# The mixer of a two-layer streaming encoder: queries, keys and convolution input turned by transposing DMAs in place of TensorE transposes

## The chip, the core and the metric

The kernel runs on one core of a Trainium2 chip. The metric is the time of one execution on the device, in microseconds (us). Times come from the device and from a hardware profile of one execution. The engines are named as in the profile: PE is TensorE, DVE is VectorE, ACT is ScalarE, POOL is GpSimd, SP is SyncE, the queue that issues nearly all DMAs here.

## What is computed

The input x has 256 tokens of 1024 features in float32. Two layers follow one another. Each layer adds half a SwiGLU block, then a mixer, then another half SwiGLU block, each with an RMS norm before and after it. The mixer has two groups of heads side by side, whose outputs are joined and projected:

```python
def _diff_attention(q, k, v, lam_vecs, subln_g, lam_init):
    ...
    q = _rope(q, S) * (DA_HEAD_DIM ** -0.5)
    k = _rope(k, S)
    ...
        s = jnp.einsum('bhcqd,bhckd->bhcqk', q_blk, k)
        ...
        p = jax.nn.softmax(jnp.where(mask, s, -jnp.inf), axis=-1)
        a = p[:, :, 0] - lam * p[:, :, 1]
        return jnp.einsum('bhqk,bhkd->bhqd', a, v)
...
def _mlstm(qk, v, o, gates, conv_w, conv_b, gate_b, norm_g):
    ...
    qk = jax.nn.silu(_causal_conv(qk, conv_w, conv_b))
    q, k = jnp.split(qk, 2, axis=-1)
```

The differential attention has 4 heads with two score maps of 64 features each. The mLSTM group convolves its q and k over 4 tokens back, and then does gated linear attention in chunks with a carried state.

What matters for the change: the projections come out with tokens on the partitions. The attention scores need q and k with features on the partitions, and so does the convolution, which shifts along tokens. So 128x128 blocks of q and k (after the rotary embedding) and of the convolution's input are turned between the projections and their use.

## The kernel before, in words

All matrix products are done in three passes on split operands (each float32 operand is a rounded high part plus a low part, `mm3`, L401 to L403). Weights are streamed: a piece of 1 MB is loaded by SP into one of three buffers `wr` (L282), and each of its two halves is split by ACT (`wh`, L288) and DVE (`wl`, L289). A buffer is free for the next load once the second half's L289 is done.

In the SwiGLU blocks the hidden activation is turned by a DMA already (`ffn_planes`, L530): ACT sorts the 16-bit halves of 128x512 floats into two planes (`planes`, L535), SP issues one transposing DMA of the planes (`turned`, L537), DVE interleaves the halves again (`hT`, L539). This happens 40 times.

The mixer (`mixer`, L703) computes six projections of 512 columns: convolution input, q, k, the mLSTM values, the attention values, the output gate, each for two tiles of 128 tokens (t = 0, 1). `traverse` (L773) writes out the order by hand: the projections are cut into 84 steps of three matmuls, and at each step the stages of the attention and mLSTM that are due there are put ahead of it. The table `AT` gives the step of each entry of the list in `stages` (L829). The order in which a step's instructions are emitted sets the order on PE; on ACT, DVE and SP a scheduler then places the instructions by their estimated times. Each engine works through its own list in order, and an instruction that waits holds up all behind it.

The turns of the mixer before the change are four 128x128 transposes on PE into a PSUM bank (`transposed`, L875, L879), and one copy out of it by ACT:

- `conv_input` (L889) evacuates the convolution's input to `nat`; `conv_input_t` (L898) turns it into `xpad`, at L899. Twice for each mixer.
- `rope` (L1052) evacuates a projection to `rv` with the norm's factor (L1057) and rotates it on DVE: `ra` = rv*cos (L1058), `rb` = swapped rv*sin (L1063), `ra` += `rb` (L1064). `roped` (L1067) turns `ra` into `qkT` at L1071, with the factor 0.125 for q. Four times for each mixer: q for t = 0, 1, then k for t = 0, 1.

These stages take part in what follows:

- `gate_rows` (L967): four PE transposes of `g2`, which DVE writes at L957; the scan `gate_chain` (L973) follows on DVE, then the convolution on DVE (L910).
- `weighted_qk` (L1018): small matmuls on PE (L1023, L1025, L1031) into three PSUM banks; DVE then reads them: `qd` (L1028), `wem` (L1027), `kwn` (L1033).
- `scores` (L1081): 16 matmuls (L1094) into two banks, then `intra_weights` (L1045) into two more. Both come from a ring of four banks called `bk`, the one that `weighted_qk` uses: the second bank of the scores, in this ring, is the one that `qd` reads.
- DVE fills the masked part (L1097) and takes the maximum (L1098), ACT takes the exponential, `combine` (L1110) subtracts on DVE (L1122) and turns the result on PE (L1124).

SBUF tiles named `nat`, `ra`, `rb`, `rv`, `planes`, `turned`, `hT` and some others share a ring of five buffers (tag `ev`), handed out in the order of emission.

## Time and profile before

| what | value |
|---|---|
| time, median of 3 runs | 963.02 us (962.27 to 963.16) |
| the profiled execution's own time | 962.02 us |
| its span, first to last instruction | 960.2 us |
| granted TensorE clock, mean | 0.999 of full speed |
| PE busy | 952.8 us, 99% of the span, 4523 instructions |
| DVE busy | 638.7 us, 67% |
| ACT busy | 571.2 us, 59% |
| DMA | 189.32 MB, mean 197 GB/s |

The span is 1.8 us shorter than the profiled execution's time, and that execution is 1.0 us under the median of the runs. Busy shares are averages over the whole span; the mixers of the two layers lie at about 195 to 275 us and about 669 to 749 us of it, and have shares of their own. In a profile's rows a line such as "L879 PE MATMUL" is a line of the kernel's code, the names are tiles without their buffer numbers, and a bracket at a row's end is the time the engine was idle just before the row and what ended that. A row that holds several instructions has their count behind an x; its time runs from the first one's start to the last one's end, and matmuls overlap one another, so that the time a matmul costs is read from the distance between starts.

### The profile page before, as it was taken

What the parts mean: (1) busy time and instruction counts of PE and PEld (TensorE: products, weight loads), DVE (VectorE), ACT (ScalarE), POOL (GpSimd) and SP (SyncE); (2) the same over time, 40 slices, a digit from 0 to 9 for tenths busy, and PEclk for the clock granted to TensorE, in tenths of its full rate; (3) what the DMA queues carried; (4) which work ended last, traced back from release to release, by engine and by line L of the source; (5) the groups of instructions that cost most, each with busy time, mean ns of one, the idle gap of its engine ahead of it and who ended that gap; (6) DMA issues with size and microseconds to landing.
All of it is one profiled execution on the core that took longest, in us unless ns stands there. A gap on an engine that the chain in (4) does not pass through costs nothing.

```text
span 960.2 us, 12037 instructions
## 1 busy us (share of the span) xinstructions
PE 952.8 (99%) x4523; PEld 788.9 (82%) x4523; DVE 638.7 (67%) x945; ACT 571.2 (59%) x937; POOL 29.5 (3%) x55
## 2 busy tenths in 40 slices
PE   9999999999999999999999999999999999999997
PEld 7888888888888888888888888888888888888885
DVE  6765655689867766555687555566988676755553
ACT  8755554577856655454476555555778466555542
POOL 2000000000010000000000000000001000000000
PEclk9999999999999999999999999999999999999999
DMA  8996656236352975676458666653454257765621
GB/s 317 328 288 202 225 193 219 105 132 241 116 192 91 299 245 193 218 247 176 154 189 283 206 225 208 196 187 128 172 202 174 90 182 256 272 205 192 225 72 44
DMA packets 69879, 189.32 MB, mean 197 GB/s; under 512 B 45274, under 2 KB 46426, under 8 KB 49086
## 3 DMA queue, kind: packets, MB, share of 16 engines
q1 hardware_dynamic: 69246, 187.95, 58.0%
q8 instruction: 35, 0.57, 0.2%
q10 hardware_dynamic: 576, 0.61, 0.2%
q14 instruction: 22, 0.18, 0.1%
HBM read 177.01 MB, written 1.05 MB: 185 GB/s over the span
## 4 chain that ended last, share of the span: by engine, by line
PE 97%; DVE 1%; DMA 1%; ACT 0%; issue 0%; POOLq 0%; DVEq 0%; ACTq 0%
PE pin L401 13%; PE pin L402 13%; PE pin L403 13%; PE bk L401 10%; PE bk L402 10%; PE bk L403 10%; PE ptr L402 6%; PE ptr L403 6%; PE ptr L401 6%; PE pin L610 1%; PE ptr L610 1%; PE ptr L879 1%; PE ptr L427 1%; DMA wr<-in_w_dram 1%; PE bk L1094 1%; PE ptr L615 1%
## 5 line engine op out<-in xcount | busy, mean ns | idle before, releaser
L289 DVE TENSOR_TENSOR wl<-wr,wh 128x1024 fp32r<-128x1024 f32 x324 | 389.2, 1221 | 180.4 <-ACT wh L288 174.4
L288 ACT ACTIVATE wh<-wr 128x1024 fp32r<-128x1024 f32 x324 | 333.9, 1055 | 171.2 <-DMA wr<-in_w_dram 44.1
L401 PE MATMUL pin<-wh,both 128*128 128x512 f32 x560 | 221.2, 396 | 0.0
L403 PE MATMUL pin<-wh,both 128*128 128x512 f32 x560 | 218.3, 390 | 0.0
L402 PE MATMUL pin<-wl,both 128*128 128x512 f32 x560 | 218.2, 390 | 0.0
L401 PE MATMUL bk<-wh,hh 128*128 128x512 f32 x352 | 137.4, 390 | 0.1
L402 PE MATMUL bk<-wl,hh 128*128 128x512 f32 x352 | 137.0, 389 | 0.0
L403 PE MATMUL bk<-wh,hl 128*128 128x512 f32 x352 | 136.9, 389 | 0.0
L403 PEld LDWEIGHTS pin<-wh,both 128*128 128x128 f32 x560 | 105.1, 188 | 22.3
L401 PEld LDWEIGHTS pin<-wh,both 128*128 128x128 f32 x560 | 105.3, 188 | 22.0 <-issue 0.7
L402 PEld LDWEIGHTS pin<-wl,both 128*128 128x128 f32 x560 | 105.3, 188 | 20.6
L403 PE MATMUL ptr<-wh,both 128*128 128x512 f32 x256 | 99.4, 389 | 0.0
L402 PE MATMUL ptr<-wl,both 128*128 128x512 f32 x256 | 99.4, 389 | 0.0
L401 PE MATMUL ptr<-wh,both 128*128 128x512 f32 x256 | 98.9, 389 | 0.0
L401 PEld LDWEIGHTS bk<-wh,hh 128*128 128x128 f32 x352 | 66.1, 188 | 14.0 <-ACT hh L550 0.5
L403 PEld LDWEIGHTS bk<-wh,hl 128*128 128x128 f32 x352 | 66.1, 188 | 13.7
L402 PEld LDWEIGHTS bk<-wl,hh 128*128 128x128 f32 x352 | 66.1, 188 | 13.5
L539 DVE COPY hT<-turned 128x1024 uint16<-128x1024 uint16 x40 | 30.3, 757 | 41.9 <-DMA turned<-planes 41.5
L401 PEld LDWEIGHTS ptr<-wh,both 128*128 128x128 f32 x256 | 48.1, 188 | 10.0
L402 PEld LDWEIGHTS ptr<-wl,both 128*128 128x128 f32 x256 | 48.1, 188 | 10.0
L550 ACT ACTIVATE hh<-hT 128x256 fp32r<-128x256 f32 x80 | 28.9, 409 | 46.0 <-DVE hT L539 46.0
L403 PEld LDWEIGHTS ptr<-wh,both 128*128 128x128 f32 x256 | 48.1, 188 | 9.9
(210 smaller groups left out, 891.9 us busy)
## 6 DMA issues: line engine op xcount, KB each, us to landing
wr<-in_w_dram SPq DMA_DIRECT2D x162, 1024.0 KB, 5.2
gpost<-in_gpost_dram SPq DMA_DIRECT2D x6, 512.0 KB, 6.3
wr<-in_w_dram SPq DMA_DIRECT2D x2, 512.0 KB, 6.1
wr<-in_w_dram SPq DMA_DIRECT2D x3, 256.0 KB, 4.3
x<-in_x_dram SPq DMA_DIRECT2D x3, 256.0 KB, 4.4
turned<-planes SPq DMA_TRANSPOSE x40, 4.4
out_dram<-x SPq DMA_DIRECT2D x2, 256.0 KB, 2.1
x<-in_x_dram SPq DMA_DIRECT2D x2, 128.0 KB, 3.0
```

The source lines that it names most:

```text
L288: ia = nc.scalar.activation(hi, raw[:, j], AF.Copy)
L289: iv = nc.vector.tensor_tensor(lo, raw[:, j], hi.bitcast(F32), op=ALU.subtract)
L401: mm(ps, xh, wh, start=start, stop=False)
L402: mm(ps, xh, wl, start=False, stop=False)
L403: mm(ps, xl, wh, start=False, stop=stop)
L427: nc.tensor.transpose(ptr[:, k, :], x[:, (4 * hf + k) * P:(4 * hf + k + 1) * P], self.ident)
L539: nc.vector.tensor_copy(hT.rearrange("p b n -> p (b n)").bitcast(U16).rearrange("p (n u) -> p u n", u=2), turned.rearrange("p (u b) n -> p ...
L550: self.nc.scalar.activation(hh, h, AF.Copy)
L610: self.nc.tensor.matmul(b, self.cols(w[kh], k)[0][:, c], both[kh][:, k].rearrange("p i t -> p (i t)"), start=kh == 0 and k == 0, stop=Fals ...
L615: self.nc.tensor.matmul(b[:, 0:NT * P], self.cols(w[kh], k)[1][:, c], both[kh][:, k, 0:NT].rearrange("p i t -> p (i t)"), start=False, sto ...
L879: self.T(ptr[:, b, :], a[:, b * P:(b + 1) * P], self.tr.ident)
L1094: self.mm(pcs[c][:, h, :], self.qkT[0][rows, h0 + h, t * P:(t + 1) * P], self.qkT[1][rows, h0 + h, 0:nk], start=True, stop=True)
```

## The change

The two helpers of the SwiGLU's turn become `turn` (ACT planes and the transposing DMA) and `joined` (the DVE copy that interleaves). The mixer uses them in place of the PE transposes: `conv_input` and `rope` end with `turn`, and `conv_input_t` and `roped` are now just the DVE copy into `xpad` or `qkT`. For each mixer this takes away 24 transposes on PE and 6 copies on ACT, and adds 6 plane sorts on ACT, 6 transposing DMAs on SP and 6 copies on DVE. The factor 0.125 of q moves into the evacuation at L1057, which needs a small product `rhalf` on DVE for each token tile. The new tiles `planes` and `turned` of the mixer come from the `ev` ring. Three stages move in the table: the turn of the convolution's input for t = 0 is now at step 10 (it was emitted ahead of step 0), q for t = 0 moves from 24 to 28, k for t = 0 from 43 to 46.

```diff
-AT = (0, 2, 6, 6, 7, 22, 24, 24, 24, 24, 36, 40, 24, 46, 34, 50, 43, 52, 52, 57, 61, 60, 61, 67, 67, 69, 71, 78, 74, 74, 78, 84)
+AT = (0, 2, 6, 6, 7, 10, 22, 24, 24, 24, 24, 36, 40, 28, 46, 34, 50, 46, 52, 52, 57, 61, 60, 61, 67, 67, 69, 71, 78, 74, 74, 78, 84)
...
     def ffn_planes(self, h):
-        nc = self.nc
-        planes = self.t2("planes", (P, 2, 512), U16)
-        nc.scalar.activation(planes, h.rearrange("p t j -> p (t j)").bitcast(U16).rearrange("p (n u) -> p u n", u=2), AF.Copy)
-        turned = self.t2("turned", (P, 8, P), U16)
-        nc.sync.dma_start_transpose(turned, planes.rearrange("p u n -> p (u n)"))
         hT = self.t2("hT", (P, 4, P))
-        nc.vector.tensor_copy(hT.rearrange("p b n -> p (b n)").bitcast(U16).rearrange("p (n u) -> p u n", u=2),
-                              turned.rearrange("p (u b) n -> p u (b n)", u=2))
+        self.joined(hT, self.turn(h.rearrange("p t j -> p (t j)")))
...
+    def turn(self, v):
+        planes = self.t2("planes", (P, 2, 512), U16)
+        self.nc.scalar.activation(planes, v.bitcast(U16).rearrange("p (n u) -> p u n", u=2), AF.Copy)
+        turned = self.t2("turned", (P, 8, P), U16)
+        self.nc.sync.dma_start_transpose(turned, planes.rearrange("p u n -> p (u n)"))
+        return turned
+
+    def joined(self, out, turned):
+        self.nc.vector.tensor_copy(out.bitcast(U16).rearrange("p b (n u) -> p u b n", u=2),
+                                   turned.rearrange("p (u b) n -> p u b n", u=2))
...
         m.part(0, 0, pins1[0], ws1[0])
-        m.conv_input_t(0)
...
             self.gate_rows,
+            lambda: self.conv_input_t(0),
             self.gate_chain,
...
-            lambda: self.roped(0, 0, 0.125),
+            lambda: self.roped(0, 0),
...
-        self.nat = nat
+        self.nat.append(tr.turn(nat))
 
     def conv_input_t(self, t):
-        self.act(self.xpad[:, :, 3 + t * P:3 + (t + 1) * P], self.transposed(self.nat), AF.Copy)
+        self.tr.joined(self.xpad[:, :, 3 + t * P:3 + (t + 1) * P], self.nat[t])
...
+        scale = self.r[t]
+        if len(self.rot) < NT:
+            scale = tr.small("rhalf", (P, 1))
+            self.ts(scale, self.r[t], 0.125, None, op0=ALU.mult)
         with tr.tc.high_priority():
-            self.rv = self.act(v, pin, AF.Copy, scale=self.r[t])
+            self.rv = self.act(v, pin, AF.Copy, scale=scale)
...
-        self.rot.append(a)
-
-    def roped(self, i, t, scale):
+        self.rot.append(tr.turn(a))
+
+    def roped(self, i, t):
...
-        self.act(self.qkT[i][:, :, t * P:(t + 1) * P], self.transposed(self.rot[2 * i + t]), AF.Copy, scale=scale)
+        self.tr.joined(self.qkT[i][:, :, t * P:(t + 1) * P], self.rot[2 * i + t])
```

How the lists change around the change is shown at three places, in the first layer's mixer. Behind the change the lines are those of the changed kernel: a few numbers higher. A bracket names the engines or DMA queues (DMAHW) that a row waits for.

The first place is DVE's list ahead of `qd`, which frees the bank that the scores wait for. `ra`, `rb` belong to the rotation of k for t = 1; `wl` are weight halves. Before:

```order
L1058 TENSOR_TENSOR ra_2136<-rv_2135,c_568 128x512 [waits Activation_49]
L1063 TENSOR_TENSOR rb_2137<-rv_2135,c_568 128x8x32 x2
L289 TENSOR_TENSOR wl_0_2324<-wr_2322,wh_0_2325 128x1024 [waits DMAHW4_49,PE_49,Activation_49]
L289 TENSOR_TENSOR wl_1_2334<-wr_2322,wh_1_2335 128x1024 [waits Activation_49]
L1064 TENSOR_TENSOR ra_2136<-ra_2136,rb_2137 128x512 [waits DVE_49]
L289 TENSOR_TENSOR wl_0_2409<-wr_2407,wh_0_2410 128x1024 [waits DMAHW5_49,Activation_49]
L1028 SCALAR_TENSOR_TENSOR qd<-qk,bk_2229 128x256 [waits PE_49]
```

And after, where `turned_2017` is q for t = 1, `turned_2114` and `turned_2149` are k for t = 0 and 1:

```order
L550 COPY qkT_2090<-turned_2017 128x2x4x128 [waits DMAHW1_49]
L1069 TENSOR_TENSOR ra_2140<-rv_2139,c_568 128x512 [waits DVE_49,Activation_49]
L1074 TENSOR_TENSOR rb_2141<-rv_2139,c_568 128x8x32 [waits DVE_49]
L1074 TENSOR_TENSOR rb_2141<-rv_2139,c_568 128x8x32
L1075 TENSOR_TENSOR ra_2140<-ra_2140,rb_2141 128x512 [waits DVE_49]
L289 TENSOR_TENSOR wl_1_2332<-wr_2320,wh_1_2333 128x1024 [waits Activation_49]
L550 COPY qkT_2211<-turned_2114 128x2x4x128 [waits DMAHW3_49]
L289 TENSOR_TENSOR wl_0_2407<-wr_2405,wh_0_2408 128x1024 [waits DMAHW0_49,Activation_49]
L550 COPY qkT_2211<-turned_2149 128x2x4x128 [waits DMAHW4_49]
L1035 SCALAR_TENSOR_TENSOR qd<-qk,bk_2232 128x256 [waits PE_49]
```

Three copies of turned halves, each of which waits for a DMA, now stand in this stretch ahead of `qd`, two of them close before it.

The second place is SP's list of the same stretch: before, the loads of weight pieces follow one another; after, the turns stand between them. Before:

```order
L282 DMA wr_2223<-in_w_dram 128x2048 [waits DMAHW7_49,DMAHW2_49,DVE_49]
L457 DMA gpost_2242<-in_gpost_dram 128x1024
L282 DMA wr_2322<-in_w_dram 128x2048 [waits DMAHW0_49,DVE_49]
L282 DMA wr_2407<-in_w_dram 128x2048 [waits DMAHW1_49,DVE_49]
L282 DMA wr_2500<-in_w_dram 128x2048 [waits DMAHW2_49,DVE_49]
L282 DMA wr_2642<-in_w_dram 128x2048 [waits DMAHW4_49,DVE_49]
```

After, with `turned_1968` and `turned_2017` for q and `turned_2114` and `turned_2149` for k:

```order
L282 DMA wr_2320<-in_w_dram 128x2048 [waits DMAHW1_49,DVE_49]
L546 DMA_TRANSPOSE turned_1968<-planes_1966 128x8x128 [waits Activation_49]
L282 DMA wr_2405<-in_w_dram 128x2048 [waits DMAHW2_49,DVE_49]
L546 DMA_TRANSPOSE turned_2017<-planes_2015 128x8x128 [waits DMAHW7_49,DMAHW3_49,Activation_49]
L282 DMA wr_2498<-in_w_dram 128x2048 [waits DMAHW4_49,DVE_49]
L546 DMA_TRANSPOSE turned_2114<-planes_2112 128x8x128 [waits Activation_49]
L546 DMA_TRANSPOSE turned_2149<-planes_2147 128x8x128 [waits DMAHW1_49,Activation_49]
L282 DMA wr_2640<-in_w_dram 128x2048 [waits DMAHW6_49,DMAHW5_49,DVE_49]
```

Each turn stands directly behind a load of 1 MB, and each load behind a turn waits in the list until that turn has been issued.

The third place is ACT's list from q for t = 1 to k for t = 1: `rv` is the evacuation of a projection, `wh` are weight halves, `qk` is the convolution's SiLU. Before:

```order
L1057 ACTIVATE rv_2099<-pin_2004,rs_191_1738 128x512 [waits PE_49]
L288 ACTIVATE wh_1_2251<-wr_2223 128x1024 [waits PE_49]
L1071 ACTIVATE qkT_2057<-ptr_2119 128x4x128 [waits PE_49]
L266 ACTIVATE qk<-conv_2038 128x1024 [waits DVE_49]
L1057 ACTIVATE rv_2135<-pin_2064,rs_204_1840 128x512 [waits PE_49]
```

And after, from the planes of q for t = 1 to those of k for t = 1:

```order
L544 ACTIVATE planes_2015<-ra_2006 128x1024 [waits DVE_49,Activation_49]
L1068 ACTIVATE rv_2104<-pin_2019,rs_191_1738 128x512 [waits PE_49]
L288 ACTIVATE wh_1_2254<-wr_2226 128x1024 [waits PE_49]
L288 ACTIVATE wh_0_2323<-wr_2320 128x1024 [waits DMAHW6_49,PE_49]
L544 ACTIVATE planes_2112<-ra_2105 128x1024 [waits DVE_49,Activation_49]
L1068 ACTIVATE rv_2139<-pin_2067,rs_206_1844 128x512 [waits DMAHW1_49]
L260 ACT_TABLE_LOAD
L288 ACTIVATE wh_1_2333<-wr_2320 128x1024 [waits PE_49]
L544 ACTIVATE planes_2147<-ra_2140 128x1024 [waits DVE_49,Activation_49]
```

The evacuation of k for t = 1 waited for PE alone as `rv_2135`. As `rv_2139` it waits for a DMA, DMAHW1, the same event that the copy out of `turned_2017` waits for on DVE: the buffer of the ring that it writes is that of the planes which the DMA of q for t = 1 still reads.

PE's list is the same at every place, without the 48 transposes.

More of the change, by code (lines that the diff above doesn't have):

```diff
@@ L765, in __init__ @@
         self.conved = None
-        self.rot, self.qkT, self.so, self.p = [], [], [], {}
+        self.nat, self.rot, self.qkT, self.so, self.p = [], [], [], [], {}
         self.aT, self.lsum, self.hn, self.y = [None] * NT, [None] * NT, [None] * NT, [None] * NT
```

6 lines of the change are left out of this document (3 added, 3 removed).

## The prediction

> **What bounds the kernel now.** I read the page first: the busy shares and the shares of the chain that ended last.
>
> ```profile
> PE 952.8 (99%) x4523; PEld 788.9 (82%) x4523; DVE 638.7 (67%) x945; ACT 571.2 (59%) x937; POOL 29.5 (3%) x55
> PE 97%; DVE 1%; DMA 1%; ACT 0%; issue 0%; POOLq 0%; DVEq 0%; ACTq 0%
> ```
>
> PE is busy all the time and carries the chain. So work taken off PE is worth its full time, as long as PE then waits for nothing. DVE's 67% is an average over the span, and the change works in the mixers alone. So I asked for the busy time by window, in the stretch from the convolution's input to `qd` of each mixer (columns: PE, PEld, DVE, ACT, POOL busy, clock, DMA share, GB/s):
>
> ```profile
> 198.60:238.30 39.70, 39.70 (x202) 32.96 (x202) 36.82 (x67) 30.93 (x45) 0.34 (x2) 1.00 0.50 182
> 672.30:712.00 39.70, 39.70 (x202) 32.96 (x202) 36.71 (x63) 30.91 (x44) 0.34 (x2) 1.00 0.50 182
> ```
>
> Here DVE has 39.70 - 36.82 = 2.9 us free, and the change puts six copies more on it. ACT has 8.8 us free. The two mixers agree within 0.1 us, so I work out the first and double it.
>
> **What is taken off PE.** PE's timeline around one group of four transposes:
>
> ```profile
> 218.59 0.40 PE L999 MATMUL bk<-c_mask,c_identr 128*128 128x512 f32 x1
> 218.82 0.60 PE L879 MATMUL ptr<-c,ra 128*128 128x128 f32 x4
> 219.18 0.48 PE L401 MATMUL pin<-wh,both 128*128 128x512 f32 x1
> 219.49 0.40 PE L402 MATMUL pin<-wl,both 128*128 128x512 f32 x1
> ...
> L879 PE MATMUL ptr<-c,ra x32: 270/272/273, 218.8 to 719.5; 128*128 128x128 f32 x32
> ```
>
> The next matmul starts 0.36 us after the group, and the one behind that 0.31 us later, where a matmul of this size takes 0.23 from start to start (218.59 to 218.82). A group costs 0.36 + 0.08 = 0.44 us; the two layers have 12 groups: 5.3 us. The duration in the last row, 272 ns for each transpose, would make that 48 x 0.272 = 13.1 us, but they overlap and the starts decide. The Trainium skill, "TensorE: Matmul & The Clock Gate", Part 4: PE-mode transpose, gives about 275 ns for a 128x128 transpose within a kernel; by it the gain would be an estimated 13.2 us. The trace agrees on the duration and not on what it costs. The six copies that leave ACT free nothing that PE waits for.
>
> **What is added.** The kernel makes the same turn 40 times in its SwiGLU blocks, so its parts have rows (the shapes are the same 128x512 floats; the copy's output is strided a little differently, and I take its price over):
>
> ```profile
> L535 ACT ACTIVATE planes<-h x40: 1037/1056/1059, 22.6 to 921.9; 128x1024 uint16<-128x1024 uint16 x40
> L539 DVE COPY hT<-turned x40: 746/755/768, 30.0 to 925.8; 128x1024 uint16<-128x1024 uint16 x40
> L537 SPq DMA_TRANSPOSE turned<-planes x40: 1237/1238/3697, 23.6 to 923.0; - x40
> DMA to landing us min/median/max: 2.7/4.4/8.9
> ```
>
> A turn alone is 1.06 + 2.7 + 0.76 = 4.5 us of delay at best, on three engines that are not PE, and 0.76 of it is DVE's. The DMA's landing is the part that varies. Behind a load of 1 MB it looks like this:
>
> ```profile
> 366.00 0.33 SPq L282 DMA_DIRECT2D wr<-in_w_dram  x1
> wr<-in_w_dram SPq DMA_DIRECT2D x1, 1024.0 KB, 5.2
> ...
> 367.64 1.24 SPq L537 DMA_TRANSPOSE turned<-planes  x1
> turned<-planes SPq DMA_TRANSPOSE x1, 4.6
> ```
>
> The load lands at 371.2, the turn at 372.2: 1.0 us after the load ahead of it, and not 2.7 after its issue. In SP's new list the turns stand just so, each behind a load. The Trainium skill, "VectorE: DVE Perf Modes", Rules for kernel authors, says to transpose 128x128 on TensorE where PSUM will do as the destination, which speaks against this change; by its table (The three transpose paths) a DMA transpose of 128x128 in bf16 takes 1309 ns, so eight of them in a row would be an estimated 10.5 us. The trace's 2.7 us for eight blocks shows that this sum does not hold here.
>
> **Where PE waits first: the gate rows.** DVE and PE around step 7:
>
> ```profile
> 198.85 2.36 DVE L289 TENSOR_TENSOR wl<-wr,wh 128x1024 fp32r<-128x1024 f32 x2 [0.25 <-ACT wh L288]
> 202.14 0.19 DVE L940 TENSOR_REDUCE gs<-bk 128x16 f32<-128x32 f32 x1 [0.93 <-PE bk L939]
> 203.36 1.22 DVE L289 TENSOR_TENSOR wl<-wr,wh 128x1024 fp32r<-128x1024 f32 x1 [0.24 <-ACT wh L288]
> ...
> 206.02 0.69 DVE L973 TENSOR_TENSOR_SCAN gt<-c_scan,bk 100x256 f32<-100x256 f32 x1
> ...
> 205.39 0.60 PE L967 MATMUL bk<-c,g 128*100 128x128 f32 x4
> ```
>
> DVE's list now has the copy into `xpad` ahead of the first of these rows and the second weight half (1.14 from start to start) ahead of `g2`, whose transposes PE makes at 205.39. That is 0.76 + 1.14 = 1.9 us more, less the 1.4 us of idle that the brackets show, plus the wait for the turn's landing (about 1 us, an estimate: the load ahead of it has to land). So `g2` is some 1.5 us late, and PE comes 0.44 early: it waits between 0.9 us (no wait for the landing) and 1.9, and I take 1.4. DVE's scan follows 1.0 us later than before. PE's wait here does not enter the sum by itself, since the next one is longer and takes it in.
>
> **Where PE waits last: `qd`.** The second bank of the scores is the one that `qd` must have read. Rows of PE, DVE and ACT ahead of it, and of the load that stands ahead of the turn of q for t = 1:
>
> ```profile
> 237.97 0.33 PE L1023 MATMUL bk<-eh,c_hotp 128*128 128x128 f32 x2
> ...
> 239.98 1.16 PE L1094 MATMUL bk<-qkT,qkT 64*128 64x128 f32 x16
> ...
> 226.45 1.22 DVE L289 TENSOR_TENSOR wl<-wr,wh 128x1024 fp32r<-128x1024 f32 x1
> ...
> 232.13 0.68 DVE L1058 TENSOR_TENSOR ra<-rv,c 128x512 f32<-128x512 f32 x1
> 232.73 0.75 DVE L1063 TENSOR_TENSOR rb<-rv,c 128x256 f32<-128x256 f32 x2
> ...
> 235.68 0.69 DVE L1064 TENSOR_TENSOR ra<-ra,rb 128x512 f32<-128x512 f32 x1
> ...
> 238.34 0.42 DVE L1028 SCALAR_TENSOR_TENSOR qd<-qk,bk 128x256 f32<-128x256 f32 x1 [0.84 <-PE bk L1023]
> ...
> 229.07 0.67 ACT L1057 ACTIVATE rv<-pin,rs 128x512 f32<-128x512 f32 x1
> ...
> 227.70 0.33 SPq L282 DMA_DIRECT2D wr<-in_w_dram  x1
> wr<-in_w_dram SPq DMA_DIRECT2D x1, 1024.0 KB, 4.9
> ```
>
> Before, DVE waits 0.84 us for PE at `qd`, so `qd` costs nothing. In the new lists a chain of turns ends there. In the times of this trace:
>
> - The weight half at 226.45 frees the buffer of the load that was issued at 227.70. It now comes after the late scan (1.0), two more copies (1.5) and one more small product (0.15): it starts at 229.1 and ends at 230.3, and the load is issued then and lands 4.9 later, at 235.2.
> - The turn of q for t = 1 stands behind that load in SP's list and lands 1.0 after it: 236.2.
> - The evacuation of k for t = 1, done at 229.7 before, now waits for just this landing, as its buffer holds the planes that the DMA reads: 236.2 + 0.67 = 236.9.
> - Its rotation on DVE takes 0.60 + 0.67 + 0.69 = 1.96: 238.9. Planes on ACT, 1.06: 239.9. The DMA with no load ahead of it in flight, 2.7: 242.6. Copy, 0.76, and `qd`, 0.42: 243.8. Seven handovers between engines at about 0.05 us (an estimate: the gap from the weight half's end at 227.67 to the load's issue is 0.03): 244.2.
>
> PE reaches the scores at 239.98 - 5 x 0.44 + 1.4 = 239.2, does the first bank, and waits until 244.2: 5.0 us. Against before it is 244.2 - 239.98 = 4.2 us late. The sixth group would give 0.44 back, but the next thing that PE does for attention is fed by DVE too:
>
> ```profile
> 247.32 1.14 DVE L1122 SCALAR_TENSOR_TENSOR p<-p,c 128x128 f32<-128x128 f32 x4
> ...
> 248.06 0.78 PE L1124 MATMUL ptr<-c,p 128*128 128x128 f32 x4
> ```
>
> These four transposes start while DVE still works on what they read, so they follow DVE, which is late by the same 4.2. The later loads of weights are late by no more than PE's use of them, so I cost them at nothing; a half that PE had to wait for would add to the shift, and is what is late next.
>
> Sum: 2 x 4.2 = +8.4 us on the profiled execution, 962.02 + 8.4 = 970.4. That execution is 1.0 under the median, so I predict 971.4. The gain of 5.3 is in this number: without it the shift would be larger only where PE waits, which is why it is lost.
>
> **Bounds of the unknown terms.** The turn of k for t = 1 can land 4.4 us after its issue (the median of the 40) in place of 2.7: +1.7 for each mixer, 974.8. Or the waits of the chain turn out shorter, down to DVE's own work. With six copies at 0.755 = 4.5 us against 2.9 us of room, `qd` starts at 238.34 + 1.6 = 239.9 and ends at 240.4 at the earliest: PE is 0.4 to 0.5 late, +0.9 for both mixers, 963.9.
>
> **The rivals.** Two are above, as bounds of one mechanism: only DVE's time counts (963.9; it holds if the buffer of the evacuation is free by 230 or so). The other rivals:
>
> - *The turns are hidden, and the kernel is faster.* Each copy is done by the time PE arrives, and nothing but the gate rows holds PE. The point that decides is `qd` of each mixer: done by 237.8 in these times, the groups come off PE whole, and the time is 963.0 - 5.3 = 957.7, or 960.5 with the gate wait of 1.4 in each mixer. For it speaks that a turn needs only 4.5 us. Against it: DVE's 2.9 us of room for 4.5 us of copies, which no earlier landing changes, unless copies overlap with the 0.93 and 0.84 us that are idle now and the weight halves move behind.
> - *The wait slows PE's clock.* After the last matmul the page's tail shows the clock:
>
> ```profile
> 953.23 0.39 PE L403 MATMUL bk<-wh,hl 128*128 128x512 f32 x1
> 956.00:957.60 1.60, 0.00 (x0) 0.00 (x0) 0.86 (x3) 0.00 (x0) 0.00 (x0) 1.00 0.42 155
> 957.70:960.20 2.50, 0.00 (x0) 0.00 (x0) 0.00 (x0) 0.00 (x0) 0.00 (x0) 0.50 0.30 98
> ```
>
>   PE ends at 953.6, and the granted clock is 1.00 until 957.6 and 0.50 from 957.7: some 4.1 us of idle PE halved it. My wait is 5.0 us. If the clock halves in it and stays so for as long as that took, 4.1 us of PE work take 2.1 more in each mixer: 971.4 + 4.2 = 975.6. Against it: the wait would have to be unbroken. The Trainium skill, "TensorE: Matmul & The Clock Gate", Part 1: The HAM clock gate, gives a window of about 3.4 us of idle before the clock is halved and about as long to restore it; by it the loss is an estimated 1.7 in each mixer. The trace's 4.1 us agrees with one such window and part of a second.
> - *The copies are dearer than 0.755 us*, as their output is strided by block: at twice that, the four copies that the chain to `qd` runs through (two into `xpad`, q and k of one token tile) make it 3.0 us longer in each mixer, 977.4. Only the stride speaks for it.
>
> **Chances.** The chain as told, with its landings between the two bounds: 0.58. DVE's time alone or little more: 0.17, at 963 to 966. The halved clock: 0.16, at 974 to 978. Hidden: 0.06. Dearer copies: 0.03. A measurement of this kernel can tell about 0.2%, 1.9 us, from no change: that is 961.1 to 964.9. Half of the second case falls within it. Faster is the hidden case, 0.06; same 0.09; slower 0.85. The range from 963.0 to 978.0 leaves out the hidden case, the dearer copies and the ends of the others.
>
> **What would show it.** In the changed kernel's profile, PE should wait at the scores (L1105) for `qd` in both mixers, about 5 us each, and 1 to 2 us at the gate rows; the chain of waits should show DMA `turned` and DVE; no L879 row should be left with `nat` or `ra`; the L550 copies should be near 0.76 us; the evacuation of k for t = 1 should wait for the landing of `turned`. The prediction is wrong in its mechanism if PE's wait at the scores ends under 2 us, or is released by anything but `qd`; it is wrong in size if the turn of q for t = 1 lands well before 236 of these times. A clock under 1.00 behind the wait would be the third case.

## The result, and the profile after

The changed kernel takes 979.02 us (median of 4 runs, 976.95 to 980.55); the kernel before, run beside it, 962.64 us (962.05 to 963.16). The ratio is 1.0169, with an interval of 1.0148 to 1.019. So it is 16.4 us slower, where the prediction had 8.4 us and ended its range at 978.0. The profiled execution took 979.52 us with a span of 977.5 us, 17.3 more than before. One execution of all the experiments, of `e10_dve_passes_only`, took 3428.67 us, far outside the other three of its kernel (968.70 to 970.10 us), and is left out of that kernel's median.

I read the page of the changed kernel first, as before: busy shares and the chain that ended last.

```profile
PE 956.0 (98%) x4475; PEld 788.8 (81%) x4475; DVE 647.2 (66%) x961; ACT 578.3 (59%) x937; POOL 31.5 (3%) x55
...
PE 91%; DVE 3%; DMA 3%; ACT 2%; issue 1%; POOLq 0%; DVEq 0%; ACTq 0%
```

48 matmul records are gone, and yet PE is busy for 3.2 us longer, which points to a slower clock. The chain now leaves PE for DVE, DMA and ACT. What PE waits for, in total, times and the longest:

```profile
PE pin L401 <- ACT rv L1068: 10.5, 4, 4.1
PE bk L974 <- DVE g L964: 3.8, 2, 2.8
```

No row has the scores and `qd`. PE waits at L401, the first matmul of a projection, for the evacuation of an earlier one (`rv`, by ACT), because the PSUM bank `pin` that it wants is the one that is evacuated. PE's timeline has the six waits (bracket: idle before), the matmul behind one of them, and the scores (L1105), which have none:

```profile
206.04 0.64 PE L974 MATMUL bk<-c,g 128*100 128x128 f32 x4 [1.03 <-DVE g L964]
223.38 0.79 PE L401 MATMUL pin<-wh,both 128*128 128x512 f32 x1 [4.14 <-ACT rv L1068]
223.97 0.63 PE L402 MATMUL pin<-wl,both 128*128 128x512 f32 x1
224.40 0.63 PE L403 MATMUL pin<-wh,both 128*128 128x512 f32 x1
...
238.81 0.51 PE L401 MATMUL pin<-wh,both 128*128 128x512 f32 x1 [2.06 <-ACT rv L1068]
...
247.81 1.16 PE L1105 MATMUL bk<-qkT,qkT 64*128 64x128 f32 x16
...
689.43 1.09 PE L974 MATMUL bk<-c,g 128*100 128x128 f32 x4 [2.78 <-DVE g L964]
707.28 0.79 PE L401 MATMUL pin<-wh,both 128*128 128x512 f32 x1 [3.35 <-ACT rv L1068]
721.96 0.51 PE L401 MATMUL pin<-wh,both 128*128 128x512 f32 x1 [0.92 <-ACT rv L1068]
```

Behind the wait of 4.14 us the matmuls start 0.43 us apart (223.97 to 224.40), where before it was 0.23. The windows behind the three longest waits show why (columns: PE, PEld, DVE, ACT, POOL busy, granted clock, DMA share, GB/s):

```profile
223.40:228.20 4.80, 4.80 (x12) 3.80 (x13) 4.80 (x13) 1.39 (x2) 0.00 (x0) 0.51 1.01 222
689.40:693.00 3.60, 3.57 (x12) 3.07 (x13) 2.36 (x6) 1.10 (x2) 0.00 (x0) 0.60 1.00 373
707.30:712.20 4.90, 4.90 (x12) 3.84 (x13) 4.90 (x13) 1.54 (x2) 0.00 (x0) 0.50 1.03 227
```

The granted clock is about halved there: 4.80 x 0.49 + 3.60 x 0.40 + 4.90 x 0.50 = 6.2 us of PE's work lost. Waits of 10.5 + 3.8 = 14.3 and this 6.2 make 20.5; the span grew by 17.3. The remainder, 3.2 us, is what the twelve groups gave back, less what is not in this sum: at the prediction's 0.44 us each they give 5.3, so some 2 us of loss are not followed here.

Why are the evacuations late? ACT's rows for q of t = 1 (222.64) and k of t = 1 (238.08):

```profile
217.34 2.08 ACT L914 ACTIVATE conv<-xpad,c 128x256 f32<-128x256 f32 x4 [0.68 <-DVE xpad L550]
219.32 1.04 ACT L544 ACTIVATE planes<-ra 128x1024 uint16<-128x1024 uint16 x1
220.27 1.05 ACT L266 ACTIVATE eE<-bk 128x512 f32<-128x512 f32 x2
221.34 1.28 ACT L260 ACT_TABLE_LOAD   x1
222.64 0.69 ACT L1068 ACTIVATE rv<-pin,rhalf 128x512 f32<-128x512 f32 x1
...
238.08 0.69 ACT L1068 ACTIVATE rv<-pin,rs 128x512 f32<-128x512 f32 x1 [2.00 <-DMA turned<-planes]
```

In the kernel before, ACT evacuated q of t = 1 right behind the matmuls, 7.7 us earlier and ahead of the convolution's products:

```profile
214.92 0.69 ACT L1057 ACTIVATE rv<-pin,rs 128x512 f32<-128x512 f32 x1 [0.30 <-PE pin L403]
```

In the changed kernel it stands in ACT's list behind the convolution's products, planes, two exponentials and a table load, 5.3 us of work that itself waits for DVE's copy into `xpad`. The evacuation of k for t = 1 waits 2.00 us for a turn to land, since its `rv` takes the buffer of planes that the DMA still reads. DVE's rows show the copies of q for t = 1 and k for t = 1, and `qd`:

```profile
238.08 0.74 DVE L550 COPY qkT<-turned 128x1024 uint16<-128x1024 uint16 x1 [1.09 <-DMA turned<-planes]
...
245.31 0.75 DVE L550 COPY qkT<-turned 128x1024 uint16<-128x1024 uint16 x1 [0.57 <-DMA turned<-planes]
246.17 0.42 DVE L1035 SCALAR_TENSOR_TENSOR qd<-qk,bk 128x256 f32<-128x256 f32 x1
```

`qd` is over at 246.59, 1.2 us before PE comes to the scores at 247.81. The chain that the prediction followed exists, but PE has been held up earlier, by evacuations that the turns made late.

### The profile page after: what moved, and what is told of

Read it like the earlier page. It is cut to its first block, busy times and chain, and to the rows that moved or that the text cites. A ratio compares the mean times of both kernels' runs of the same rounds, so it can differ in the third digit from the quotient of the medians.

```text
span 977.5 us, 11988 instructions
## 1 busy us (share of the span) xinstructions
PE 956.0 (98%) x4475; PEld 788.8 (81%) x4475; DVE 647.2 (66%) x961; ACT 578.3 (59%) x937; POOL 31.5 (3%) x55
## 4 chain that ended last, share of the span: by engine, by line
PE 91%; DVE 3%; DMA 3%; ACT 2%; issue 1%; POOLq 0%; DVEq 0%; ACTq 0%
PE pin L401 12%; PE pin L402 11%; PE pin L403 11%; PE bk L401 10%; PE bk L403 10%; PE bk L402 10%; PE ptr L401 6%; PE ptr L403 6%; PE ptr L402 6%; DMA turned<-planes 3%; DVE wl L289 2%; PE pin L617 2%; PE ptr L617 2%; PE ptr L427 1%; PE pin L622 1%; PE ptr L622 1%
## 5 line engine op out<-in xcount | busy, mean ns | idle before, releaser
L289 DVE TENSOR_TENSOR wl<-wr,wh 128x1024 fp32r<-128x1024 f32 x324 | 388.8, 1221 | 181.7 <-ACT wh L288 175.4
L401 PE MATMUL pin<-wh,both 128*128 128x512 f32 x560 | 223.7, 400 | 10.5 <-ACT rv L1068 10.5
L402 PE MATMUL pin<-wl,both 128*128 128x512 f32 x560 | 220.5, 394 | 0.0
L403 PE MATMUL pin<-wh,both 128*128 128x512 f32 x560 | 220.3, 393 | 0.0
L401 PE MATMUL bk<-wh,hh 128*128 128x512 f32 x352 | 137.4, 390 | 0.0
L401 PEld LDWEIGHTS pin<-wh,both 128*128 128x128 f32 x560 | 106.8, 191 | 34.6 <-ACT rv L1068 12.2
L403 PEld LDWEIGHTS pin<-wh,both 128*128 128x128 f32 x560 | 106.6, 190 | 22.9
L401 PE MATMUL ptr<-wh,both 128*128 128x512 f32 x256 | 99.0, 389 | 0.0
L403 PEld LDWEIGHTS bk<-wh,hl 128*128 128x128 f32 x352 | 66.1, 188 | 13.8
L401 PEld LDWEIGHTS bk<-wh,hh 128*128 128x128 f32 x352 | 66.1, 188 | 13.5
L401 PEld LDWEIGHTS ptr<-wh,both 128*128 128x128 f32 x256 | 48.1, 188 | 9.9
```

What stands on the lines that cost most here:

```text
L289: iv = nc.vector.tensor_tensor(lo, raw[:, j], hi.bitcast(F32), op=ALU.subtract)
L401: mm(ps, xh, wh, start=start, stop=False)
L402: mm(ps, xh, wl, start=False, stop=False)
L403: mm(ps, xl, wh, start=False, stop=stop)
```

## The experiments

In the experiments the kernel before, run on the same chips, had medians of 961.7 to 962.6 us. A diff shows only the lines that decide, against the changed kernel unless the text names another; helpers that pass an instruction on are left out. The theory that I started with was that four late evacuations and the slower clock behind them are the whole loss. The rivals were that DVE's added work costs the time wherever PE happens to wait, and that the DMA's traffic or ACT's planes do.

### Parts of the change

**The convolution's input back on PE** (both of its turns), q and k by DMA:

```diff
-        self.nat.append(tr.turn(nat))
+        self.nat.append(nat)
...
-        self.tr.joined(self.xpad[:, :, 3 + t * P:3 + (t + 1) * P], self.nat[t])
+        self.act(self.xpad[:, :, 3 + t * P:3 + (t + 1) * P], self.transposed(self.nat[t]), AF.Copy)
```

> The changed kernel with one part undone: the convolution's input is turned on PE again (its two groups of transposes and two copies by ACT, at their old places), q and k by DMA. Bank theory (PE loses its time where a late evacuation holds a PSUM bank that the next projection needs, and where the clock halves behind such a wait): the gate rows' waits (1.03 and 2.78 us) and the 1.4 us of halved clock behind the second go; the evacuation of q for t=1 stands ahead of the exponentials and the table load on ACT again, so the waits of 4.14 and 3.35 us at step 24 shrink to about 1 each and the 4.7 us of halved clock behind them go; four groups of transposes come back, 1.8. That is 979.0 - 3.8 - 1.4 - 5.5 - 4.7 + 1.8 = 965 us, 963 to 968. The rival (what matters is the chain of turns that ends at qd, as predicted): the chain is left but for the late scan, 969 to 975 us.

Measured: 976.66 us, ratio 1.0152 (1.0134 to 1.017). A miss by 12 us, and not clear of the changed kernel, whose interval (1.0148 to 1.019) overlaps. The waits at the gate rows are gone, but the waits for evacuations have grown from 10.5 to 13.8 us. ACT's rows show what holds up the evacuation of k for t = 1 here:

```profile
236.51 1.06 ACT L544 ACTIVATE planes<-ra 128x1024 uint16<-128x1024 uint16 x1 [3.75 <-DVE ra L1075]
237.47 0.67 ACT L1068 ACTIVATE rv<-pin,rs 128x512 f32<-128x512 f32 x1
```

The planes of k for t = 0 stand ahead of it in ACT's list and wait 3.75 us for DVE's rotation. So a DVE that is behind reaches PE through ACT's list too.

**q and k back on PE**, the convolution's input by DMA:

```diff
-        self.rot.append(tr.turn(a))
+        self.rot.append(a)
...
-        self.tr.joined(self.qkT[i][:, :, t * P:(t + 1) * P], self.rot[2 * i + t])
+        self.act(self.qkT[i][:, :, t * P:(t + 1) * P], self.transposed(self.rot[2 * i + t]), AF.Copy, scale=(0.125, 1.0)[i])
```

> The other part undone: q and k are turned on PE again with the factor 0.125 at the copy, the convolution's input by DMA. Bank theory: only the waits at the gate rows stay (1.0 and 2.8 us, and 1.4 of halved clock behind the second), less 1.8 us for four groups of transposes: 962.6 + 5.2 - 1.8 = 966 us, 964 to 968. The rival that all of the loss comes from q and k and the convolution's turn is hidden: 962.6 - 1.8 = 961 us.

Measured: 969.13 us, ratio 1.0064 (1.0049 to 1.0079), above both forecasts. PE waits 3.7 us in all at the gate rows, and 2.7 us at k's transposes for k's rotation. The second wait was not expected: the two copies into `xpad` stand well ahead of that rotation on DVE, and it is late all the same, behind two convolution products and two weight halves (`wl`), where the kernel before has one half.

### Following the wait

**The evacuation of q for t = 1 ahead of the convolution's products** in ACT's list, else the changed kernel:

```diff
+            i = self.act(conv[:, b, :], self.xpad[:, b, 0:S], AF.Identity, scale=tr.convw[:, l, b, 0:1],
+                         bias=tr.convb[:, l, b:b + 1])
+            tr.after(i, [self.rot_q])
...
+            if len(self.rot) < NT:
+                self.rot_q = self.rv
```

> The changed kernel, all turns by DMA, with one rule of order more: on ACT the convolution's four operations come behind the evacuation of q for t=1, which so comes ahead of the exponentials and the table load. Bank theory: the waits at step 24 fall from 4.14 and 3.35 us to under 1 us each and the halved clock behind them (2.2 and 2.5 us) goes, about 11 us less: 968 us, 966 to 972 (up, where the next wait, for the evacuation of k for t=1, grows in turn). The rival (the turns' chain to qd sets the end): no change, 977 to 981 us.

Measured: 980.43 us, ratio 1.0186 (1.0171 to 1.0201). PE's timeline has the wait at that place cut to 0.82 us, and the next one grown from 2.06 to 5.98:

```profile
220.13 0.50 PE L401 MATMUL pin<-wh,both 128*128 128x512 f32 x1 [0.82 <-ACT rv L1069]
...
237.94 0.79 PE L401 MATMUL pin<-wh,both 128*128 128x512 f32 x1 [5.98 <-ACT rv L1069]
```

The wait moved on. PE arrives earlier, and what the next evacuation hangs on is not earlier.

**PE kept busy in the wait** by 14 matmuls on data that nobody uses, so that the clock stays:

```diff
...
+            if s == 24:
+                tr.warm(14, bank=tr.bank_tr())
```

> The changed kernel with 14 idle matmuls (bf16, 512 columns of ones into a bank that nobody reads, 3.2 us) put in front of step 24, where PE waits 4.14 and 3.35 us. Nothing else is changed. If the halved clock behind these waits is what costs 2.2 and 2.5 us: the wait that is left is under 1 us, the clock stays full, and the time is 4.7 us lower, 974 us (972 to 976). If the slower matmuls behind the waits have another cause (or the waits alone count): 979 us, or more where the idle matmuls delay the work.

Measured: 982.5 us, ratio 1.0209 (1.0192 to 1.0226): no gain. The wait left at this place is 1.07 us, with the clock at full speed behind it; the next wait is 3.49 us, and behind that one the clock is 0.66 over 5 us. A clock that is saved in one place is lost in the next.

**The first copy into `xpad` behind `g2`** on DVE, for the gate rows alone:

```diff
...
+        i = self.tr.joined(self.xpad[:, :, 3 + t * P:3 + (t + 1) * P], self.nat[t])
+        if t == 0:
+            self.tr.after(i, [self.g2w])
```

> The changed kernel with one rule of order: the copy into xpad for t=0 comes on DVE behind the two operations that write g2, so that the gate rows do not wait for a landing. The waits at the gate rows (1.0 and 2.8 us) and the halved clock behind the second (1.4) go. If what follows on DVE and ACT comes earlier by as much: 974 us (972 to 976). Rival, that the wait moves on to step 24: 978 to 981 us.

Measured: 976.79 us, ratio 1.0158 (1.0142 to 1.0173), between the two forecasts and not clear of the changed kernel. The gate rows now cost 0.44 us in each mixer, the waits for evacuations are 11.2 us in all.

**A ring of their own for the evacuations.** `rv` leaves the ring of five that planes and turns use for another of the same pool (to make room, `mh` moves to a third):

```diff
-    TAGS = {"kwn": ("kwn", 1), "aT0": ("aT0", 1), "aT1": ("aT1", 1)}
-    for _n in ("nat", "ra", "rb", "rv", "tmp", "y", "so", "xg", "h", "planes", "turned", "hT"):
+    TAGS = {"kwn": ("kwn", 1), "mh": ("junk", 2), "aT0": ("aT0", 1), "aT1": ("aT1", 1)}
+    for _n in ("nat", "ra", "rb", "tmp", "y", "so", "xg", "h", "planes", "turned", "hT"):
```

> The changed kernel, all turns by DMA, with the evacuations rv taken out of the ring of five buffers that planes and turned share (they go to another ring of four, and the small tile mh to a scratch ring). On ACT the evacuations of q and k for t=1 then wait for PE alone and stand ahead of the planes of t=0. Ring theory (the evacuations are late because their buffer and their place on ACT hang on a turn): no wait of PE at step 24 or at the projections' banks any more; the gate rows' 3.8 + 1.4 us stay, and the scores now wait for the copy of k by some 2 us in each mixer: 962.6 - 5.3 + 5.2 + 4 = 966.5, 964 to 971 us. Rival (DVE has no room for the six copies, and the loss only moves on to the next place, as it did in the three experiments before): 974 to 980 us.

Measured: 975.29 us, ratio 1.0141 (1.0123 to 1.0158), the rival's number; its interval overlaps that of the changed kernel. Its waits, and the window of the first mixer (columns as above):

```profile
PE bk L1105 <- DVE qkT L550: 11.1, 2, 6.0
```

```profile
198.50:243.40 44.90, 38.94 (x188) 31.72 (x185) 42.95 (x79) 34.93 (x46) 0.34 (x2) 1.00 0.70 210
```

No wait for an evacuation is left. PE now waits at the scores, for DVE's copy of k into `qkT`, and DVE is busy for 42.95 of the 44.90 us. So the ring held the evacuations up, and behind it stands another cause: DVE.

**Both, and on ACT the planes of q and of k behind the evacuation for t = 1** (the own ring, the copy behind `g2`, and this):

```diff
...
-        self.rot.append(tr.turn(a))
+        self.rot.append(a)
+        if t:
+            for n in (-2, -1):
+                self.rot[n] = tr.turn(self.rot[n])
+                tr.after(tr.planes, [self.rv])
```

> All turns by DMA; the ring of e5, the copy behind g2 of e6, and the planes of t=0 of q and of k on ACT behind the evacuation of t=1. Ring theory: the waits at the gate rows and at the projections' banks are both gone, and only the scores wait, by some 2 us in each mixer (more by 1 to 2 for k, whose planes come later): 962 us, 959 to 966. Rival (no room on DVE): 972 to 978 us.

Measured: 971.0 us, ratio 1.0096 (1.0082 to 1.0109). Better by 4.3 than e5, between the two forecasts, and 9 over the first: 9.3 us of wait at the scores for the copy of k are left.

### Each suspect by itself

**DVE's work alone.** The kernel before, with its transposes, and behind each of the six copies of ACT in a mixer one more pass of DVE over the result, in place, in the 16-bit pattern of the joining copy. No planes, no DMA:

```diff
+    def again(self, out):
+        out = out.bitcast(mybir.dt.uint16).rearrange("p b (n u) -> p u b n", u=2)
+        self.tr.nc.vector.tensor_copy(out, out)
```

> The kernel before, all turns on PE, with a DVE copy of each turned block onto itself added (six in each mixer, the same 128x1024 16-bit form, about 0.75 us each), between ACT's copy and the use. No turn by DMA, no planes. DVE theory: DVE has 2.9 us of room for 4.5, k's rotation gets 2 us or more late, PE waits for it and for the copies at the scores: 967 us, 965 to 972. Rival (the latency of the turns, not DVE's time, makes the loss): under 963.5 us.

Measured: 969.01 us, ratio 1.0076 (1.006 to 1.0093), as the theory had it. So 12 passes of 0.78 us, 9.4 us on an engine that is busy 67% of the span, cost 7.3 us. The waits are 4.4 us at the transposes of k for t = 0, with a slower clock behind one of the two. DVE's rows ahead of them show the place: a pass and two pieces of other work that are not needed yet stand ahead of the last step of k's rotation (L1066).

```profile
231.57 0.78 DVE L1079 COPY qkT<-qkT 128x1024 uint16<-128x1024 uint16 x1
232.22 0.49 DVE L912 SCALAR_TENSOR_TENSOR conv<-xpad,c,conv 128x256 f32<-128x256 f32 x1
232.60 1.24 DVE L289 TENSOR_TENSOR wl<-wr,wh 128x1024 fp32r<-128x1024 f32 x1
233.74 0.71 DVE L1066 TENSOR_TENSOR ra<-ra,rb 128x512 f32<-128x512 f32 x1
```

**Planes and DMAs alone.** The kernel before, with its transposes, and the planes and the transposing DMA of each of the six turns beside them, whose result nobody reads:

```diff
         self.nat = nat
+        tr.turn(nat)
...
         self.rot.append(a)
+        tr.turn(a)
```

> The kernel before, with all its transposes, and beside them the planes and the transposing DMA of the six turns in each mixer, whose result nobody reads: so the change's load on ACT, on SP and on the ring of five buffers, without a copy on DVE and without anything that PE could wait for in a turn. Theory (DVE): nearly free, 962 to 964.5, since ACT has 8.8 us to spare in the stretch. Rival (ACT's order, the ring and the queue cost something by themselves): 967 or more, with PE waits for evacuations or for k's rotation that have no DVE copy ahead of them. With e10_dve_passes_only (969.55) the two halves of the change's load then stand side by side.

Measured: 980.44 us, ratio 1.0188 (1.0174 to 1.0202). I expected it to be nearly free. It costs 18 us, no less than the whole change, without a single copy on DVE. The waits and ACT's rows:

```profile
PE pin L401 <- ACT rv L1064: 11.7, 2, 5.8
```

```profile
221.67 2.06 ACT L914 ACTIVATE conv<-xpad,c 128x256 f32<-128x256 f32 x4
223.64 0.58 ACT L266 ACTIVATE eE<-bk 128x512 f32<-128x512 f32 x1
224.22 1.28 ACT L260 ACT_TABLE_LOAD   x1
225.51 0.60 ACT L1079 ACTIVATE qkT<-ptr 128x512 f32<-128x512 f32 x1
226.01 0.68 ACT L1064 ACTIVATE rv<-pin,rs 128x512 f32<-128x512 f32 x1
```

It is the evacuation of q for t = 1 again, behind the convolution's products, and one wait of 5.84 us in each mixer. Behind it the clock is 0.50 over 5 us in the first mixer (from 226.7) and 0.67 over 5 us in the second (from 710.5). The waits, 11.7 us, with 2.5 and 1.7 of PE's work lost and 1.4 of waits at the gates and at q's transposes, make 17.3 of the 18.

**The same with the own ring** for `rv`, against e14 (the edit of e5, with `mh` moved too, and nothing else):

```diff
-    TAGS = {"kwn": ("kwn", 1), "aT0": ("aT0", 1), "aT1": ("aT1", 1)}
-    for _n in ("nat", "ra", "rb", "rv", "tmp", "y", "so", "xg", "h", "planes", "turned", "hT"):
+    TAGS = {"kwn": ("kwn", 1), "mh": ("junk", 2), "aT0": ("aT0", 1), "aT1": ("aT1", 1)}
+    for _n in ("nat", "ra", "rb", "tmp", "y", "so", "xg", "h", "planes", "turned", "hT"):
```

> e14_turn_unread (980.44: planes and turns that nobody reads) with one thing changed: the evacuations `rv` no longer share the ring of five buffers with planes and turns (the rings of e5_rv_other_ring). In e14 PE waits 5.84 us in each mixer for the evacuation of q for t = 1, which stands on ACT behind the convolution's products, two exponentials, a table load and a copy. Theory: it stands there because its buffer of the ring is handed on late; with a buffer of its own it is taken early in ACT's list, the waits go, the clock stays, and 962 to 965 are left, which says that the planes and the transposing DMAs cost nothing by themselves. Rival: ACT and the DMA traffic cost time whatever the ring: over 970.

Measured: 964.04 us, ratio 1.0019 (1.001 to 1.0028). Some 16 of the 18 us are gone, as the theory had it. The evacuation of q for t = 1 is early in ACT's list now:

```profile
216.08 0.69 ACT L1064 ACTIVATE rv<-pin,rs 128x512 f32<-128x512 f32 x1 [0.30 <-PE pin L403]
220.21 2.07 ACT L914 ACTIVATE conv<-xpad,c 128x256 f32<-128x256 f32 x4
```

ACT and the DMA queue do the same work in both kernels. So planes and DMAs cost 1.8 us by themselves (0.0019 of the time; by the interval 1.0 to 2.7); the other 16 came with the shared ring. That the evacuation gets its buffer late there, and so a late place in ACT's list, is the reading that fits; `mh` was not moved alone.

### The place on DVE

**q alone by DMA**, own ring, the convolution's input and k on PE:

```diff
...
-        self.rot.append(tr.turn(a))
+        self.rot.append(tr.turn(a) if len(self.rot) < NT else a)
...
+        if i == 0:
+            self.tr.joined(self.qkT[i][:, :, t * P:(t + 1) * P], self.rot[2 * i + t])
+        else:
+            self.act(self.qkT[i][:, :, t * P:(t + 1) * P], self.transposed(self.rot[2 * i + t]), AF.Copy)
```

> Only q is turned by DMA (two turns in each mixer); the convolution's input and k on PE as before; rv in the other ring as in e5. DVE has 2.9 us of room for two copies, 1.5 us, and q is needed late. Ring theory: nothing waits, four groups of transposes are saved: 962.6 - 1.8 = 960.8 us, 960 to 962. Rival (every copy on DVE in this stretch is paid for): 963 to 966 us.

Measured: 969.36 us, ratio 1.0074 (1.0061 to 1.0086), above both forecasts. PE waits 6.6 us for k's rotation at k's transposes. DVE's rows show one of q's copies inside that rotation, with a weight half behind it:

```profile
232.02 0.73 DVE L550 COPY qkT<-turned 128x1024 uint16<-128x1024 uint16 x1
232.65 1.21 DVE L289 TENSOR_TENSOR wl<-wr,wh 128x1024 fp32r<-128x1024 f32 x1
233.78 0.68 DVE L1075 TENSOR_TENSOR ra<-ra,rb 128x512 f32<-128x512 f32 x1
```

**The same, q's copies on POOL** in place of DVE, against e8:

```diff
+            self.tr.joined(self.qkT[i][:, :, t * P:(t + 1) * P], self.rot[2 * i + t], self.tr.nc.gpsimd)
```

> As e8 (only q by DMA), with the two copies that interleave the halves on POOL, which is idle here, in place of DVE. DVE theory (the copies' 0.76 us each come ahead of k's rotation, which PE needs just in time): the waits of 2.9 and 3.7 us at the transposes of k for t=0, and the halved clock behind them, go; four groups of transposes are saved and nothing is paid: 960.5 us, 959.5 to 963. Rival (it is the order on ACT and the DMAs that make k late, or POOL's copies slow DVE down by as much): 966 to 970 us.

Measured: 970.56 us, ratio 1.009 (1.0075 to 1.0105). Just above the rival's range, but not a clean test, as one more weight half also came ahead of k's rotation on DVE. The group of POOL's copies, and DVE's rows while POOL worked from 224.00 to 228.32 and from 229.21 to 231.27:

```profile
L550 POOL COPY qkT<-turned 128x1024 uint16<-128x1024 uint16 x4 | 11.1, 2776 | 44.5 <-DMA turned<-planes 44.3
```

```profile
225.87 1.22 DVE L289 TENSOR_TENSOR wl<-wr,wh 128x1024 fp32r<-128x1024 f32 x1
227.00 1.93 DVE L917 SCALAR_TENSOR_TENSOR conv<-xpad,c,conv 128x256 f32<-128x256 f32 x2
...
229.99 1.77 DVE L1069 TENSOR_TENSOR ra<-rv,c 128x512 f32<-128x512 f32 x1
```

The last product takes 0.68 us elsewhere (e12's rows, below), the two before it 0.87 together in e12. In the second mixer two of the convolution's products take 3.00 us beside the copies. So the four copies cost DVE some 4.3 us in this way, where they would have taken it 4 x 0.75 = 3.0 themselves.

**The same, q's copies on DVE behind k's rotation** for t = 0, against e8:

```diff
-            self.tr.joined(self.qkT[i][:, :, t * P:(t + 1) * P], self.rot[2 * i + t])
+            c = self.tr.joined(self.qkT[i][:, :, t * P:(t + 1) * P], self.rot[2 * i + t])
+            self.tr.after(c, [self.turned])
...
-AT = (0, 2, 6, 6, 7, 22, 24, 24, 24, 24, 36, 40, 28, 46, 34, 50, 43, 52, 52, 57, 61, 60, 61, 67, 67, 69, 71, 78, 74, 74, 78, 84)
+AT = (0, 2, 6, 6, 7, 22, 24, 24, 24, 24, 36, 40, 41, 46, 41, 50, 43, 52, 52, 57, 61, 60, 61, 67, 67, 69, 71, 78, 74, 74, 78, 84)
```

> Only q is turned by DMA, as in e8_q_only (969.36), but q's two copies stand behind k's rotation for t = 0 in DVE's list, and not ahead of it. Theory (DVE's place): what cost e8 its 6.6 us of wait at k's transposes was that the copies and the halves moved with them stood ahead of k's rotation. Here two weight halves still stand ahead of the last add of that rotation, one more than in the kernel before, so about 1 us of wait is left in each mixer at those transposes; four groups of transposes go at 0.44 each: 961 to 964. Rival (DVE's total): each copy is paid for wherever it stands, since DVE has nothing to spare up to the scores; then the wait only moves to qd or to the masks behind it, and the time stays at 967 to 970.

Measured: 963.65 us, ratio 1.0015 (1.0006 to 1.0025), as the theory had it. DVE's rows:

```profile
229.32 0.68 DVE L1069 TENSOR_TENSOR ra<-rv,c 128x512 f32<-128x512 f32 x1
...
232.86 0.68 DVE L1075 TENSOR_TENSOR ra<-ra,rb 128x512 f32<-128x512 f32 x1
...
236.59 1.38 DVE L550 COPY qkT<-turned 128x1024 uint16<-128x1024 uint16 x2
...
239.24 0.42 DVE L1035 SCALAR_TENSOR_TENSOR qd<-qk,bk 128x256 f32<-128x256 f32 x1 [0.18 <-PE bk L1030]
```

Both copies stand behind the rotations, `qd` even waits for PE, and the rotation of k for t = 0 ends at 233.54. PE waits 1.6 us for it in each mixer, where it was 2.89 and 3.70 in e8, and the clock stays. The same copies at another place on the same engine are worth 5.7 us (0.0059 of the time).

**k's transposes three steps later** as well, against e12:

```diff
-AT = (0, 2, 6, 6, 7, 22, 24, 24, 24, 24, 36, 40, 41, 46, 41, 50, 43, 52, 52, 57, 61, 60, 61, 67, 67, 69, 71, 78, 74, 74, 78, 84)
+AT = (0, 2, 6, 6, 7, 22, 24, 24, 24, 24, 36, 40, 41, 46, 41, 50, 46, 52, 52, 57, 61, 60, 61, 67, 67, 69, 71, 78, 74, 74, 78, 84)
```

> e12_q_late (963.65) with k's transposes for t = 0 three steps later (46 in place of 43, about 2 us of PE work), so that k's rotation, which was 1.6 us late for them in each mixer, is there in time. Theory: the 1.6 us go, but one more weight half now stands ahead of q's copies and of qd on DVE, so that PE may wait up to 0.9 us at the scores: 962.2 (960.4 to 963.7). Rival: the wait moves to the scores whole, and the time stays at 963.6 or rises.

Measured: 961.41 us, ratio 0.9994 (0.9986 to 1.0003): no difference from the kernel before. The wait at k's transposes is gone, and 0.8 us in all are left, at matmuls that wait for `kwn`. So four groups off PE, with nothing but this wait left behind them, bring at most 1.3 us (0.0014 of the time).

### All six turns

**All copies on POOL**, with the own ring and the planes as in e7, against e7:

```diff
-        self.tr.joined(self.qkT[i][:, :, t * P:(t + 1) * P], self.rot[2 * i + t])
+        self.tr.joined(self.qkT[i][:, :, t * P:(t + 1) * P], self.rot[2 * i + t], self.tr.nc.gpsimd)
```

> As e7 (all turns by DMA, the evacuations in another ring), with all six copies of each mixer on POOL. DVE theory: DVE gets its 4.5 us back, the waits at the scores shrink from 4.1 and 5.2 us to 2 or less, and the halved clock behind them goes: 962 us, 959 to 966 (more, if a copy takes POOL over 2 us). Rival (the turns' latency alone makes the wait at the scores): 970 us or more.

Measured: 973.33 us, ratio 1.0119 (1.0102 to 1.0136), the rival's number: 10.8 us of wait at the scores for POOL's copies of k. POOL's copies of q and k take 1.61 us in the mean.

**All six by DMA, as in e7, with q's copies late** as in e12 (and at step 41), against e7:

```diff
...
-        self.tr.joined(self.qkT[i][:, :, t * P:(t + 1) * P], self.rot[2 * i + t])
+        c = self.tr.joined(self.qkT[i][:, :, t * P:(t + 1) * P], self.rot[2 * i + t])
+        if i == 0:
+            self.tr.after(c, [self.turned])
```

> e7_ring_and_order (971.0: all six turns by DMA, own ring for rv, first copy behind the gates) with q's two copies behind k's rotation for t = 0, as in e12. Theory (place on DVE): the 4.1 and 5.2 us that PE waited at the scores for k's copy fall to 1 to 2, since k's rotation is no longer held up by the copies of q, and the time falls to 963 to 967. Rival (the turn of k is too long a way in any case: planes, DMA and copy after a rotation that is just in time): the waits at the scores stay over 3 us, 969 to 972.

Measured: 978.31 us, ratio 1.0168 (1.0155 to 1.0182). Neither theory's number. The waits and ACT's row of k's planes:

```profile
PE bk L1113 <- DVE qkT L550: 17.2, 2, 8.8
```

```profile
240.41 2.15 ACT L544 ACTIVATE planes<-ra 128x1024 uint16<-128x1024 uint16 x2 [0.30 <-DVE ra L1077]
```

The planes of k for t = 0 are made together with those for t = 1, at 240.41, though the rotation of t = 0 ended at 234.6. By these rows ACT's list held k's turn back, so the kernel does not tell what DVE's would have done. Whether some order makes all six turns as cheap as PE's transposes stays open; I tried no other.

## Why the prediction was wrong, point by point

- **"A group costs 0.36 + 0.08 = 0.44 us."** Right in size. e12 has four groups less, 3.2 us of waits at a full clock and 1.36 us more time: 1.8 us for four groups, 0.46 each. e16, with 0.8 us of waits and 0.65 us less time, gives 0.36; both are estimates, with intervals wider than their difference. The Trainium skill's rule that the prediction cited from "VectorE: DVE Perf Modes", Rules for kernel authors (transpose on TensorE), is borne out here by the times of all these kernels: none with turns by DMA is measurably faster than the one with transposes.
- **The gate rows, "between 0.9 us and 1.9, and I take 1.4".** 1.03 and 2.78 us. The second is outside, and the clock behind it was 0.60 over 3.6 us. That "the next one is longer and takes it in" did not hold either: in e6, with 2.9 us less of these waits, those for evacuations grow by 0.7 only.
- **The turn's parts.** The copies took 0.74 to 0.76 us as predicted (0.755), and the evacuation of k for t = 1 does wait for the landing of q's turn. That came at 238.0 in place of 236.2, and `qd` ended at 246.59 in place of 244.2. The dearer copies are ruled out.
- **The step that failed: "PE reaches the scores at 239.98 - 5 x 0.44 + 1.4 = 239.2, does the first bank, and waits until 244.2".** PE reaches them at 247.81, and `qd` is over at 246.59. The prediction had the late evacuation in its hands ("the evacuation of k for t = 1 ... now waits for just this landing") and followed what is made from it, the rotation, the planes, the copy and `qd`. It did not follow what the evacuation sets free: the PSUM bank that PE's next projection writes. That hold comes 9 us before the scores. And it looked at ACT's list for k alone: the evacuation of q for t = 1 had also moved, behind 5.3 us of other work, and gave the longest wait of all, 4.14 us. By the prediction's own test ("released by anything but `qd`") the mechanism was wrong.
- **"The wait slows PE's clock", at 0.16.** It did, three times, but none of them at the scores: 6.2 us in all, where the rival had 4.2. The rule in the Trainium skill, "TensorE: Matmul & The Clock Gate", HAM oscillation — how this bites in real kernels, allows gaps of up to about 3.4 us; the trace does not agree, as the wait of 2.78 us was enough to halve the clock.
- **"ACT has 8.8 us free" and DVE "2.9 us".** DVE's bound was meant as the mild case (963.9). e10 shows 969.01 for DVE's work alone, since the list puts a pass ahead of the end of k's rotation, which had been just in time (done at 232.2 for transposes at 232.7 in the kernel before). ACT's spare time was real (e15), but its list has an order, and the ring decided that order.
- **The sum.** Two causes, each of which makes a kernel slower by itself: the shared ring (e14 against e15: some 16 us) and the place of copies on DVE (e10: 7.3 us; e8 against e12: 5.7). They do not add up: together 16.4 us, and with the ring mended (e5) still 13.5. That a PE held by the one gives time to the other would explain it; no run shows that by itself. e5 comes near the prediction's wait (5.1 and 6.0 us at the scores, where it had 5.0) and near the time of its rival with the halved clock (975.29, where it had 975.6), but there PE waits for k's copy and no evacuation waits, so the agreement is luck.

## What to carry to other kernels

When a buffer's holder is late, follow both ends of it: what is made from its content, and who waits for the place that it leaves, a PSUM bank above all. Where an engine is full on the way to a deadline, the price of an added instruction is read from its place in that engine's list and not from the engine's free time: the same two copies in each mixer cost 5.7 us more ahead of the deadline's work than behind it. And before new tiles join a ring of buffers, ask which early evacuation shares it; taking one tile out of the ring was worth 16 us in e14's kernel, and in the changed one about 3 us, which the runs do not tell clearly from nothing.
